# Attention scores of a hybrid encoder block: the queries' high by the keys' low parts over 64 rows of TensorE, two blocks of queries in two halves of its rows

## The chip, the cores and the metric

The kernel runs on one core of a Trainium2 chip. The metric is the device time of one execution in microseconds. A core has five engines that work side by side and wait for one another by semaphores: TensorE (PE in the profile; its weight loads are listed apart, as PEld), VectorE (DVE), ScalarE (ACT), GpSimd (POOL) and SyncE (SP), which issues most DMA transfers. A matrix product on TensorE has a stationary operand, loaded first, of up to 128 rows (the dimension summed over) by 128 columns, and a moving operand of the same rows and up to 512 columns, which streams through. Products are written to PSUM, in banks of 512 f32 a partition.

## What is computed

One layer of a streaming encoder on 512 frames of width 1024: attention and a gated recurrence side by side, merged, then a feed-forward part. The change lies in the attention alone: 16 heads of 64, where each frame sees its own chunk of 64 and the eight chunks before it.

```python
def chunked_band_attention(q, k, v, rel_table):
    ...
    scale = 1.0 / math.sqrt(HEAD_DIM)
    s = jnp.einsum('bnqhd,bnkhd->bhnqk', q, kb).astype(jnp.float32) * scale
    s = s + rel_bias_band(rel_table).astype(jnp.float32)[None, :, None, :, :]
    ...
    s = jnp.where(valid[None, None, :, None, :], s, NEG_INF)
    p = jax.nn.softmax(s, axis=-1).astype(v.dtype)
    o = jnp.einsum('bhnqk,bnkhd->bnqhd', p, vb)
    return o.reshape(B, S, D_ATTN)
```

q, k and v are columns of one projection of the normalised input. All is in float32.

## The kernel before

**High and low parts.** Every matrix product is made of products in the type fp32r. Each operand is split into a high part (the value rounded to fp32r) and a low part (what is left), and a product of two values is high by high, plus high by low, plus low by high; in the big projections (`mm3`, L74) these are three instructions on 128 rows.

**The scores use the rows differently.** A head has only 64 dimensions, so 128 rows hold two things. `q_tile` (L817) projects the queries of two heads (a pair `pr`; head 2·pr+e has the index e) and lays out a tile `q` of 128 x 2 x 512: for head e the rows `own` (0 to 63 for e = 0, 64 to 127 for e = 1) hold the high part of the scaled query, the rows `other` hold its low part. `k_tile` (L828) makes two such tiles: `kh` with the keys' high part in both halves of the rows, `kl` with their low part in both. One product of `q` with `kh` over 128 rows therefore gives high by high plus low by high; one of `q` with `kl` gives high by low plus low by low.

**Scores of a head** (`scores`, L862). The 512 queries are four blocks of 128. Block qb sees the first (qb+1)·128 keys, so its products have 128, 256, 384 and 512 columns. `products(qb)` issues two instructions, L878 with `kh` and L879 with `kl`, into the same place in PSUM. Blocks 0 and 1 share one bank (`low`), block 2 has a bank of the pool `mm` (four banks, used by the projections too), block 3 the second bank with the tag `s`. The products run one block ahead of the softmax: VectorE adds the bias and takes the negative maximum (L887), ScalarE takes the exponential with its sum (L888). After all four blocks VectorE inverts the sums (L889) and GpSimd scales the four blocks (L891).

**Order of the work.** `scores(h + 1)` stands between the transposes of head h's probabilities (`transposed`, L894; ten of 128x128 at L902) and some projections of later heads or gates (`laid`, L934), then the weighting of the values (`weigh`, L911; eight products at L922). So head h+1's softmax runs beside these projections, and TensorE needs the result when it comes to the next transposes. Within this loop TensorE's order is the order of the program (`manual_schedule`); the order on the other engines is made by a planner from its own estimates of durations. Scores of head 0 are issued earlier, while the recurrent branch's output is projected (L950).

**Room.** Tiles of the attention lie in the pools `aw` (values, biases, queries and keys of odd pairs; opened at L846, closed at L978) and `aw2` (probabilities; closed at L965). After that the pool `wo` for part of the output projection's weights is opened (L966). A tile that lies where an older one lay waits until the older one has been read. `halves(e)` (L807) gives the slices `own` and `other`.

Of the kernel before, what the change touches and what calls it, by code (L numbers as in the profile page):

```python
# [9 lines left out]
F32R = mybir.dt.float32r  # L10
# [4 lines left out]
P = 128  # L15
D = 1024
S = 512
KT = D // P
NT = S // P
# [19 lines left out]
def block_kernel(ctx: ExitStack, tc: tile.TileContext, x, norm_mix_g, w_in, b_merge, rel_table,  # L39
# [3 lines left out]
    pe, dve, act, pool, sp = nc.tensor, nc.vector, nc.scalar, nc.gpsimd, nc.sync  # L43

    def pool_of(name, bufs=1, side="left"):
        return tc.tile_pool(name=name, bufs=bufs, side=side, reuse_waits="tile")

    def opened(name, bufs=1, side="left"):
        st = ExitStack()
        return st, st.enter_context(pool_of(name, bufs, side))  # L50
# [17 lines left out]
    def f(ap):  # L68
        return ap.bitcast(F32)

    def mm_tile(name, tag="mm"):
        return ps.tile([P, S], F32, tag=tag, bufs=4 if tag == "mm" else 2, name=name)
# [12 lines left out]
    def split_pair(o, src):  # L85
        split(o[:, 0], o[:, 1], src)
# [249 lines left out]
    def weights(name, ahead=1):  # L336
        prefetch(index[name] + 1 + ahead)
        if index[name] + 1 == len(made):
            low_parts()
        return made[index[name]]  # L340

    def project(o, whl, c, xs, lo=0, hi=S):

        n = len(xs)
        for k in range(n):
            at = slice(c * P, (c + 1) * P)
            mm3(o[:, lo:hi], whl(0, k, at), whl(1, k, at),
                xs[k][:, 0, lo:hi], xs[k][:, 1, lo:hi], k == 0, k == n - 1)
# [165 lines left out]
    low, high = slice(0, S), slice(S, D)  # L514
# [135 lines left out]
    def bias_tile(h):  # L650
        b = aw.tile([P, S], F32, tag="bias", bufs=2, name=f"bias{h}")
        src = ext_d[h:h + 1, 0:S]
        band = bass.AP(tensor=src.tensor, offset=src.offset, ap=[[1, P], [1, S]])
        sp.dma_start(out=b[:], in_=band)
        pool.memset(b[64:128, 448:512], NEG)
        return b
# [144 lines left out]
    def blocks(ap):  # L801
        return ap.rearrange("p (b i) -> p b i", i=P)

    def backwards(ap):
        return blocks(ap)[:, :, ::-1]

    def halves(e):  # L807
        own, other = slice(e * HD, e * HD + HD), slice(HD - e * HD, 2 * HD - e * HD)
        return own, other


    qk = {}

    def qk_pool(pr):
        return aw if pr % 2 else qkp

    def q_tile(pr):  # L817
        po = mm_tile(f"po_q{pr}")
        project(po, weights(f"qk{pr}"), 0, xnT)
        q = qk_pool(pr).tile([P, 2, S], F32R, tag="qk", bufs=3, name=f"q{pr}")  # L820
        for e in range(2):
            own, other = halves(e)
            src = backwards(po[own, :])
            act.activation(blocks(q[own, e]), src, AF.Copy, scale=0.125)
            dve.scalar_tensor_tensor(blocks(q[other, e]), src, 0.125, blocks(f(q[own, e])), ALU.mult, ALU.subtract)
        qk[pr] = [q]

    def k_tile(pr):  # L828
        po = mm_tile(f"po_k{pr}")
        project(po, weights(f"qk{pr}"), 1, xnT)  # L830
        kh = qk_pool(pr).tile([P, 2, S], F32R, tag="qk", bufs=3, name=f"kh{pr}")
        kl = qk_pool(pr).tile([P, 2, S], F32R, tag="qk", bufs=3, name=f"kl{pr}")
        for e in range(2):
            own, other = halves(e)
            act.activation(kh[own, e], po[own, :], AF.Copy)
            dve.tensor_sub(kl[own, e], po[own, :], f(kh[own, e]))
            act.activation(kh[other, e], po[own, :], AF.Copy)
            pool.tensor_copy(kl[other, e], kl[own, e])
        qk[pr] += [kh, kl]

    q_tile(0)
    k_tile(0)
    rw2_stack.close()
    rw_stack.close()
    aw2_stack, aw2 = opened("aw2", 2)
    aw_stack, aw = opened("aw", 2, "right")  # L846


    vs = {}
# [11 lines left out]

    def scores(h):  # L862
        pr, e = divmod(h, 2)
        q, kh, kl = qk[pr]
        bias = bias_tile(h)
        lsum = cp.tile([P, NT], F32, tag="lsum", bufs=2, name=f"l{h}")
        nmax = cp.tile([P, NT], F32, tag="nmax", bufs=2, name=f"m{h}")
        rl = cp.tile([P, NT], F32, tag="rl", bufs=2, name=f"rl{h}")
        prob = [aw2.tile([P, (qb + 1) * P], F32, tag=f"p{qb}", name=f"p{h}_{qb}") for qb in range(NT)]

        low = ps.tile([P, S], F32, tag="s", bufs=2, name=f"s{h}_01")
        scs = [low[:, 0:P], low[:, 256:512], mm_tile(f"s{h}_2"), ps.tile([P, S], F32, tag="s", bufs=2, name=f"s{h}_3")]

        def products(qb):
            w = (qb + 1) * P
            sc = scs[qb][:, 0:w]
            qs = q[:, e, qb * P:(qb + 1) * P]
            pe.matmul(sc, qs, kh[:, e, 0:w], start=True, stop=False, skip_group_check=qb < 2)  # L878
            pe.matmul(sc, qs, kl[:, e, 0:w], start=False, stop=True, skip_group_check=qb < 2)  # L879

        products(0)
        for qb in range(NT):
            w = (qb + 1) * P
            if qb < NT - 1:
                products(qb + 1)

            dve.tensor_tensor_reduce(prob[qb][:], scs[qb][:, 0:w], bias[:, S - w:S], -1.0, 3e38, ALU.add, ALU.min, nmax[:, qb:qb + 1])  # L887
            act.activation(prob[qb][:], prob[qb][:], AF.Exp, bias=nmax[:, qb:qb + 1], scale=-1.0, accum_out=lsum[:, qb:qb + 1])  # L888
        dve.reciprocal(rl[:], lsum[:])  # L889
        for qb in range(NT):  # L890
            pool.tensor_scalar(prob[qb][:], prob[qb][:], rl[:, qb:qb + 1], 1.0, ALU.mult, ALU.mult)  # L891
        return prob
# [41 lines left out]
    def laid(h):  # L934
        m, at = divmod(h, 4)
        qs, ks, va = (lambda pr: lambda: q_tile(pr)), (lambda pr: lambda: k_tile(pr)), (lambda t: lambda: v_tile(m + 1, t))
        if h >= 12:
            return [lambda: gate(0, h - 8)], []
        first_, second = 2 * m + 2, 2 * m + 3
        return {0: (([qs(1), ks(1)] if m == 0 else []) + ([] if m == 0 else [qs(first_)]), [qs(first_)] if m == 0 else []),  # L940
                1: ([ks(first_)], [va(0)]),
                2: ([va(1), va(2)], [va(3)]),
                3: ([qs(second)], [ks(second)])}[at]
# [4 lines left out]
    for j in range(KT):  # L948
        if j == 6:
            prob = scores(0)  # L950
        po = mm_tile(f"po_yb{j}")
        project(po, weights(f"yb{j - j % 2}"), j % 2, rnn)
        dve.scalar_tensor_tensor(zB[j], zB[j], 1.0, po[:], ALU.add, ALU.mult)
    with tc.manual_schedule(engines={mybir.EngineType.PE}):
        for h in range(HEADS):
            pp = transposed(h, prob)
            if h + 1 < HEADS:
                prob = scores(h + 1)
            before, after = laid(h)
            for what in before:  # L960
                what()
            weigh(h, pp)
            for what in after:
                what()
    aw2_stack.close()  # L965
    wo_stack, wop = opened("wo", 4)  # L966
    extra["wo1"] = wop
    barrier[0] = "fg2"
# [3 lines left out]
    for j in range(KT):  # L972
# [2 lines left out]
        dve.scalar_tensor_tensor(ta[j], ta[j], 1.0, py[:], ALU.add, ALU.mult)  # L975
        dve.tensor_add(ta[j], ta[j], zB[j])
        split_pair(mT[j], ta[j])
    aw_stack.close()  # L978
    z_stack.close()
    qk_stack.close()  # L980
    rnn_stack.close()
# [25 lines left out]
    for t in range(NT):  # L1007
# [11 lines left out]
        q = cp.tile([P, 1], F32, tag="ssq", bufs=4, name=f"hsq{t}")  # L1019
# [64 lines left out]
    sc_stack, sc = opened("sc", 2)  # L1084
# [138 lines left out]
    with tc.manual_schedule(engines={mybir.EngineType.PE, mybir.EngineType.DVE}):  # L1223
# [3 lines left out]
        for i in plain:  # L1227
            w = weights(f"fo0_{i}", 3)
# [4 lines left out]
        for n, i in enumerate(paired):  # L1233
            w = weights(f"fo0_{i}", 4)
# [20 lines left out]
        for n, i in enumerate(paired):  # L1255
            w = weights(f"t12_{i}", 4)
# [8 lines left out]
        w = weights(f"fo1_{plain[-3]}", 5)  # L1265
# [75 lines left out]
```

## Time and profile before

| | |
|---|---|
| median of 3 runs | 871.99 us (871.76 to 872.05) |
| profiled execution | 872.03 us |
| its span, first to last instruction | 870.3 us |
| TensorE busy / weight loads busy | 861.0 us / 766.4 us |
| VectorE / ScalarE / GpSimd busy | 599.4 / 488.5 / 100.6 us |
| DMA | 96.39 MB, 111 GB/s in the mean |

Times in the profile are microseconds from the start of the span unless marked ns. A row of the timeline has the start, the duration, the engine, the line of the program, the operation, what is written and read, and the shapes; in brackets stands how long the engine was idle before it, and what ended that. For a product, `128*128 128x512` means 128 rows by 128 columns of weights and a result of 128 partitions by 512. A row of groups gives the count, the busy time, the mean length in ns, then the idle time ahead of the group and who ended it. Products overlap in TensorE's pipeline, so the distance from start to start, and not the length, is what one of them takes of the stream.

### The profile page before, as it was taken

The page shows a single profiled execution, that of the slowest core. Times are in us where ns is not written, and L with a number is a line of the kernel's source. Part 1 is how long each engine was busy: PE and PEld are TensorE (multiplying, and loading weights), DVE is VectorE, ACT ScalarE, POOL GpSimd, SP SyncE. Part 2 cuts the span into 40 slices and gives each one's busy share as a digit, 9 for nine tenths or more (in the row PEclk, how much of TensorE's full clock was granted, in tenths as well). Part 3 has the DMA queues.
Part 4 walks back from the last instruction along what each step waited for, and adds up shares of the span by engine and source line. Part 5 has one row for each costly group of instructions (what it writes and reads, how often), then busy time and mean ns, then how long its engine had stood idle before and what let it go on. Part 6 is the DMA issues. An engine that isn't in the chain of part 4 may idle for free.

```text
span 870.3 us, 13342 instructions
## 1 busy us (share of the span) xinstructions
PE 861.0 (99%) x5130; PEld 766.4 (88%) x5130; DVE 599.4 (69%) x947; ACT 488.5 (56%) x863; POOL 100.6 (12%) x166
## 2 busy tenths in 40 slices
PE   9999999999999999999999999999999999999997
PEld 7988888888889889898888889999999999888885
DVE  5676557563357576775556656988888888698895
ACT  7685546652347576666633366556555556545434
POOL 3602111220012232222200000000000001000000
PEclk9999999999999999999999999999999999999999
DMA  8133223423323232232122802423333332426542
GB/s 285 60 121 97 84 86 97 123 97 96 108 83 89 73 106 89 74 106 76 49 98 101 286 29 72 144 97 122 115 105 97 98 98 76 153 99 233 180 133 96
DMA packets 88735, 96.39 MB, mean 111 GB/s; under 512 B 5744, under 2 KB 74960, under 8 KB 88672
## 3 DMA queue, kind: packets, MB, share of 16 engines
q1 hardware_dynamic: 87072, 92.03, 33.1%
q10 hardware_dynamic: 1232, 2.95, 0.9%
q8 instruction: 40, 0.66, 0.3%
q0 software_dynamic: 368, 0.57, 0.2%
q14 instruction: 23, 0.19, 0.1%
HBM read 93.39 MB, written 2.14 MB: 110 GB/s over the span
## 4 chain that ended last, share of the span: by engine, by line
PE 95%; DVE 2%; DMA 1%; POOL 1%; issue 1%; ACT 0%; SPq 0%; ACTq 0%; DVEq 0%; POOLq 0%
PE po_out L76 2%; PE po_out L77 2%; PE po_out L78 2%; PE p_fu L78 2%; PE p_fg L78 2%; PE p_fg L77 2%; PE p_fg L76 2%; PE p_fu L76 2%; PE p_fu L77 2%; PE pT L902 2%; PE o L922 2%; PE po_v L76 2%; PE po_v L78 2%; PE po_v L77 2%; PE po_xr L77 2%; PE po_gr L78 2%
## 5 line engine op out<-in xcount | busy, mean ns | idle before, releaser
L891 POOL TENSOR_SCALAR p<-p,rl 128x128 f32<-128x128 f32 (+1 forms) x64 | 36.7, 592 | 134.8 <-DVE rl L889 134.5
L888 ACT ACTIVATE p<-p,m 128x128 f32<-128x128 f32 (+1 forms) x64 | 35.7, 560 | 12.1 <-DVE m L887 11.9
L1112 POOL TENSOR_TENSOR act_lo<-act,act_hi 128x1024 fp32r<-128x1024 f32 x1 | 2.4, 2403 | 300.7 <-ACT act_hi L1111 300.7
L76 PE MATMUL po_v<-whl_v,xnT 128*128 128x256 f32 x128 | 36.5, 285 | 0.0
L78 PE MATMUL po_v<-whl_v,xnT 128*128 128x256 f32 x128 | 36.2, 283 | 0.0
L77 PE MATMUL po_v<-whl_v,xnT 128*128 128x256 f32 x128 | 36.2, 283 | 0.0
L76 PE MATMUL po_out<-whl_fo,act_hi 128*128 128x512 f32 (+1 forms) x80 | 30.8, 385 | 0.5 <-ACT c_u L370 0.5
L77 PE MATMUL po_out<-whl_fo,act_hi 128*128 128x512 f32 (+1 forms) x80 | 30.7, 384 | 0.0
L78 PE MATMUL po_out<-whl_fo,act_lo 128*128 128x512 f32 (+1 forms) x80 | 30.7, 384 | 0.0
L83 DVE TENSOR_TENSOR whl_qk<-raw_qk,whl_qk 128x1024 fp32r<-128x1024 f32 x16 | 20.9, 1304 | 13.4 <-ACT whl_qk L82 13.4
L887 DVE CUSTOM_DVE_ANT_0 p<-s,bias 128x128 f32<-128x128 f32 (+1 forms) x64 | 29.1, 484 | 1.0 <-PE s L879 1.0
L83 DVE TENSOR_TENSOR whl_fu_s<-s_fu,whl_fu_s 128x1024 fp32r<-128x1024 f32 x20 | 24.1, 1222 | 6.2 <-ACT whl_fu_s L82 6.2
L83 DVE TENSOR_TENSOR pp<-pT,pp 128x384 fp32r<-128x384 f32 (+1 forms) x48 | 27.6, 597 | 0.5 <-ACT pp L82 0.4
L77 PE MATMUL po_xr<-xnT,whl_xr 128*128 128x512 f32 (+1 forms) x80 | 27.7, 353 | 0.1
L77 PE MATMUL po_gr<-xnT,whl_gr 128*128 128x512 f32 (+1 forms) x80 | 27.5, 347 | 0.0
L78 PE MATMUL po_gr<-xnT,whl_gr 128*128 128x512 f32 (+1 forms) x80 | 27.3, 347 | 0.0
L78 PE MATMUL po_xr<-xnT,whl_xr 128*128 128x512 f32 (+1 forms) x80 | 27.2, 346 | 0.0
L76 PE MATMUL po_gr<-xnT,whl_gr 128*128 128x512 f32 (+1 forms) x80 | 27.2, 347 | 0.0
L83 DVE TENSOR_TENSOR whl_fg_s<-s_fg,whl_fg_s 128x1024 fp32r<-128x1024 f32 x20 | 24.0, 1223 | 4.1 <-ACT whl_fg_s L82 4.0
L82 ACT ACTIVATE whl_qk<-raw_qk 128x1024 fp32r<-128x1024 f32 x16 | 16.9, 1054 | 17.5 <-PE po_yb L78 10.4
L76 PE MATMUL po_xr<-xnT,whl_xr 128*128 128x512 f32 (+1 forms) x80 | 26.3, 351 | 0.3 <-ACT xnT L564 0.2
L76 PE MATMUL po_k<-xnT,whl_qk 128*128 128x512 f32 x64 | 25.2, 393 | 0.0
(498 smaller groups left out, 3258.9 us busy)
## 6 DMA issues: line engine op xcount, KB each, us to landing
raw_fg<-in_w_ffn_in_dram SPq DMA_DIRECT2D x24, 512.0 KB, 4.2
raw_fu<-in_w_ffn_in_dram SPq DMA_DIRECT2D x22, 512.0 KB, 3.6
raw_qk<-in_w_in_dram SPq DMA_DIRECT2D x32, 256.0 KB, 3.2
raw_fo<-in_w_ffn_out_dram SPq DMA_DIRECT2D x16, 512.0 KB, 3.6
raw_xr<-in_w_in_dram SPq DMA_DIRECT2D x8, 512.0 KB, 4.2
raw_gr<-in_w_in_dram SPq DMA_DIRECT2D x8, 512.0 KB, 4.1
raw_ga<-in_w_in_dram SPq DMA_DIRECT2D x8, 512.0 KB, 3.7
raw_gb<-in_w_in_dram SPq DMA_DIRECT2D x8, 512.0 KB, 3.4
```

Source lines behind the costliest of these rows:

```text
L76: pe.matmul(o, sh, mh, start=start, stop=False, skip_group_check=parts)
L77: pe.matmul(o, sh, ml, start=False, stop=False, skip_group_check=parts)
L78: pe.matmul(o, sl, mh, start=False, stop=stop, skip_group_check=parts)
L82: act.activation(hi, src, AF.Copy)
L83: dve.tensor_sub(lo, src, f(hi))
L887: dve.tensor_tensor_reduce(prob[qb][:], scs[qb][:, 0:w], bias[:, S - w:S], -1.0, 3e38, ALU.add, ALU.min, nmax[:, qb:qb + 1])
L888: act.activation(prob[qb][:], prob[qb][:], AF.Exp, bias=nmax[:, qb:qb + 1], scale=-1.0, accum_out=lsum[:, qb:qb + 1])
L891: pool.tensor_scalar(prob[qb][:], prob[qb][:], rl[:, qb:qb + 1], 1.0, ALU.mult, ALU.mult)
L902: pe.transpose(pt[:, at * P:(at + 1) * P], prob[qb][:, kb * P:(kb + 1) * P], ident[:])
L922: pe.matmul(po[:, S - n:S], st, pp[i][:, part, lo:lo + n], start=kb == 0 and part == 0, stop=kb == NT - 1 and part == 1)
L1112: (dve if i else pool).tensor_sub(lo[:], o[:], f(hi[:]))
```

## The change

Queries' high parts are multiplied by keys' low parts over the 64 rows that hold them, instead of all 128, so the product of the two low parts is no longer computed. For block 3 a copy of the queries' high parts, `qh`, is made in the other half of the rows by GpSimd (two copies of 64x128 a pair of heads), and its product uses the other half of TensorE's rows; the low keys are in both halves already. The four high products of a head now come first, then the low ones in the order of blocks 0, 1, 3, 2, and the softmax of the four blocks after all eight. As blocks 0 and 1 share a bank, the high product of block 1 no longer carries the start mark. The pool `aw` is closed before `wo` is opened.

```diff
+        if pr:
+            q_other(pr)
+
+    def q_other(pr):
+
+        q = qk[pr][0]
+        qh = aw.tile([P, P], F32R, tag="qh", bufs=2, name=f"qh{pr}")
+        for e in range(2):
+            own, other = halves(e)
+            pool.tensor_copy(qh[other, :], q[own, e, S - P:S])
+        qhs[pr] = qh
...
     aw_stack, aw = opened("aw", 2, "right")
+    q_other(0)
...
-        q, kh, kl = qk[pr]
+        (q, kh, kl), qh = qk[pr], qhs[pr]
+        own, other = halves(e)
...
-        def products(qb):
-            w = (qb + 1) * P
-            sc = scs[qb][:, 0:w]
-            qs = q[:, e, qb * P:(qb + 1) * P]
-            pe.matmul(sc, qs, kh[:, e, 0:w], start=True, stop=False, skip_group_check=qb < 2)
-            pe.matmul(sc, qs, kl[:, e, 0:w], start=False, stop=True, skip_group_check=qb < 2)
-
-        products(0)
+        def cols_of(qb):
+            return slice(qb * P, (qb + 1) * P)
+
+        def high(qb):
+
+            w = (qb + 1) * P
+            pe.matmul(scs[qb][:, 0:w], q[:, e, cols_of(qb)], kh[:, e, 0:w], start=qb != 1, stop=False, skip_group_check=True)
+
+        def low_(qb, rows, qs):
+
+            w = (qb + 1) * P
+            pe.matmul(scs[qb][:, 0:w], qs, kl[rows, e, 0:w], start=False, stop=True, skip_group_check=True)
+
+        for qb in range(NT):
+            high(qb)
+
+        low_(0, own, q[own, e, cols_of(0)])
+        low_(1, own, q[own, e, cols_of(1)])
+        low_(3, other, qh[other, :])
+        low_(2, own, q[own, e, cols_of(2)])
         for qb in range(NT):
             w = (qb + 1) * P
-            if qb < NT - 1:
-                products(qb + 1)
...
     aw2_stack.close()
+    aw_stack.close()
     wo_stack, wop = opened("wo", 4)
...
-    aw_stack.close()
     z_stack.close()
```

More of the change, by code (lines that the diff above doesn't have):

```diff
@@ L809, in halves @@
         return own, other
-    qk = {}
+    qk, qhs = {}, {}
     def qk_pool(pr):
```

## The prediction, made before the changed kernel ran

> **What bounds the kernel now.** I read the page first: its spans and busy times, then the chain of waits. One execution was profiled: 870.3 us of span, 872.03 us as timed, so 1.7 us lie around the span. That execution stands 0.04 us above the median of the runs (871.99), so a sum made on it holds for the median as it is.
>
> ```profile
> span 870.3 us, 13342 instructions
> PE 861.0 (99%) x5130; PEld 766.4 (88%) x5130; DVE 599.4 (69%) x947; ACT 488.5 (56%) x863; POOL 100.6 (12%) x166
> PE 95%; DVE 2%; DMA 1%; POOL 1%; issue 1%; ACT 0%; SPq 0%; ACTq 0%; DVEq 0%; POOLq 0%
> ```
>
> PE (TensorE) is 95% of the chain that ended last. So a microsecond taken from its stream is a microsecond of the kernel, unless PE then waits for somebody. The windows view over heads 1 to 15 of the attention, and the list of what PE waited for, say how near such waits are:
>
> ```profile
> 244.80:432.00 187.20, 186.31 (x1110) 165.94 (x1108) 122.86 (x269) 123.70 (x270) 44.98 (x87) 1.00 0.29 86
> PE pT L902 <- POOL p L891: 0.9, 3, 0.3
> ```
>
> The columns of the first row are length, then PE, PEld, DVE, ACT, POOL. In 187.20 us PE is idle for 0.89, and that is three waits of at most 0.3 us of the transposes (L902) for POOL's scaled probabilities (L891).
>
> The timeline of PE and of its weight loads (PEld) over one head's scores shows what is to be changed. Columns: start, duration, engine and line.
>
> ```profile
> 304.64 0.19 PEld L878 LDWEIGHTS s<-kh,q 128*128 128x128 f32 x1
> 304.67 0.30 PE L878 MATMUL s<-kh,q 128*128 128x128 f32 x1
> 304.81 0.28 PE L879 MATMUL s<-kl,q 128*128 128x128 f32 x1
> 304.86 0.19 PEld L878 LDWEIGHTS s<-kh,q 128*128 128x128 f32 x1
> 304.93 0.33 PE L878 MATMUL s<-kh,q 128*128 128x256 f32 x1
> 304.98 0.19 PEld L879 LDWEIGHTS s<-kl,q 128*128 128x128 f32 x1
> 305.09 0.28 PE L879 MATMUL s<-kl,q 128*128 128x256 f32 x1
> 305.21 0.34 PE L878 MATMUL s<-kh,q 128*128 128x384 f32 x1
> 305.38 0.33 PE L879 MATMUL s<-kl,q 128*128 128x384 f32 x1
> 305.56 0.39 PE L878 MATMUL s<-kh,q 128*128 128x512 f32 x1
> 305.79 0.40 PE L879 MATMUL s<-kl,q 128*128 128x512 f32 x1
> 305.79 0.19 PEld L76 LDWEIGHTS po_q<-xnT,whl_qk 128*128 128x128 f32 x1
> 306.02 0.40 PE L76 MATMUL po_q<-xnT,whl_qk 128*128 128x512 f32 x1
> ```
>
> Three things are to be seen. From start to start the eight take 0.14, 0.12, 0.16, 0.12, 0.17, 0.18, 0.23 and 0.23 us: 1.35 us a head. A product of 512 columns holds the stream 0.23 us, one of 384 takes 0.17 to 0.18, but one of 128 takes no less than one of 256: 0.12 us, the spacing of the loads (304.86, 304.98), is a floor for each product. And a product is 0.39 us long though its follower starts after 0.23: 0.16 us of it is a tail that the next one covers.
>
> **The change part by part.** *Columns.* The products by the keys' high parts stay at 128 rows, the low ones go to 64; all eight remain, each with its load. The four high ones in a row: 0.14 + 0.12 + 0.17 + 0.23 = 0.66 us. The low ones: 0.12 (block 0), 0.12 (block 1), then block 3 on the other half of the rows and block 2 on its own half. One after the other these two take 0.23 + 0.18 = 0.41. Side by side, with the second begun one load spacing after the first, they take 0.12 + 0.18 = 0.30 (block 3 is through after 0.23). So a head takes 1.20 us where they run together, a gain of 0.15; 1.31 where they don't, a gain of 0.04. Over 16 heads that is -2.4 or -0.6 us. No row shows two products in two halves, so these are the ends that I have for it; I take -2.4, because the only thing that both would need, a load 0.12 after the other, is what the rows show for every pair. If the load for the free half could also be drawn ahead, blocks 1 and 3 would start together: 0.12 + 0.12 + 0.18 = 0.42 instead of 0.54, and -4.3 us.
>
> *The change of rows.* Each head now goes from 128 rows to 64 and back. The trace has one product with few rows, at the start, in the timeline of PE:
>
> ```profile
> 7.57 0.22 PE L464 MATMUL gm_p<-ident,gm_r 8*128 8x8 f32 x1
> 7.72 0.33 PE L562 MATMUL pt_mix_0t<-ident,xs_mix 128*128 128x128 f32 x1
> 7.88 0.27 PE L562 MATMUL pt_mix_0s<-ident,xs_mix 128*128 128x128 f32 x1
> 7.99 0.27 PE L562 MATMUL pt_mix_2t<-ident,xs_mix 128*128 128x128 f32 x1
> ```
>
> The 8-row product ends at 7.79, the 128-row one behind it at 8.05: 0.26 us from end to end. The next two ends, 8.15 and 8.26, are 0.10 and 0.11 apart. So 0.15 us more at the change, which is nearly the tail of 0.16; part of it may be a wait for the data of the second, so this is no proof. Bounds: 0 a change, if the tail is covered as now; 0.16, if the array runs empty first; and if the next weights are not drawn ahead either, another 0.12 to 0.19 (a load's spacing, a load's length). I take 0.15, the row that it is nearest to: 2 x 16 x 0.15 = +4.8 us (0 to 11).
>
> On this the Trainium skill (TensorEngine Tiling, Key Properties) says that a change of tiling mode, unlike a change of tile, drains TensorE. By that alone the term would be the full tail, 2 x 16 x 0.16 = 5.1 us, against 4.8 by the row. The skill (TensorE: Matmul & The Clock Gate, Part 3) also says that a weight load overlaps a running product only where their rows differ; in this trace it does so with the same 128 rows (the load at 304.98 lies inside the product of 304.93), so the measurement decides and the loads of blocks 0, 1 and 2 keep their 0.12.
>
> *The softmax behind it.* The low products used to come right after the high ones; now four high ones go first. VectorE's reduction of block 0 waits for PE:
>
> ```profile
> 305.51 0.29 DVE L887 CUSTOM_DVE_ANT_0 p<-s,bias 128x128 f32<-128x128 f32 x1 [0.34 <-PE s L879]
> 306.07 1.22 DVE L83 TENSOR_TENSOR whl_v<-raw_v,whl_v 128x1024 fp32r<-128x1024 f32 x1
> 310.66 0.18 DVE L889 RECIPROCAL rl<-l 128x4 f32<-128x4 f32 x1
> 311.40 2.05 POOL L891 TENSOR_SCALAR p<-p,rl 128x128 f32<-128x128 f32 x4
> 313.51 0.98 PE L902 MATMUL pT<-ident,p 128*128 128x128 f32 x7 [0.29 <-POOL p L891]
> ```
>
> It began 0.14 us after the end of the second low product (305.09 + 0.28). That one now starts at 304.67 + 0.66 + 0.12, with one row change 0.15 later, and ends at 305.88; the reduction begins at 306.02, 0.51 us late (0.36 without the row change). In this head, and in the two others that wait, VectorE is occupied from there to the reciprocal, POOL follows, and PE stands 0.29 us for the last block. If VectorE keeps its order, the chain moves by 0.51, and PE itself comes 0.15 later (+0.30 for two changes, -0.15 for the overlap): +0.36 a wait. If the planner puts the weight split of 306.07 first, whose cover is 1.22 us, the lateness is gone: -0.15. For three heads -0.45 to +1.1; I take +0.4. No other head's transposes wait (the row of waits counts three).
>
> *POOL, memory, and what costs nothing.*
>
> ```profile
> L838 POOL CAST kl<-kl 64x512 fp32r<-64x512 f32 x16 | 9.8, 610 | 57.9 <-DVE kl L836 57.8
> L655 POOL MEMSET bias<- 64x64 f32 x16 | 2.3, 147 | 9.9 <-DMA bias<-ext_d 9.1
> L82 ACT ACTIVATE whl_wo<-raw_wo x8: 1061/1062/1066, 466.2 to 490.5; 128x1024 fp32r<-128x1024 f32 x8
> L922 PE MATMUL o<-pp,v x128: 220/309/398, 258.1 to 435.8; 128*128 128x512 f32 x32, 128*128 128x384 f32 x32, 128*128 128x256 f32 x32, 128*128 128x128 f32 x32
> ```
>
> The copies of block 3's queries are 16 of 64x128; between a memset of 64x64 (0.147) and a cast of 64x512 (0.610) that is 2.4 to 9.8 us of POOL. They lie in its idle time (45 of 187 us are busy) and are read by the scores two or more steps later, so 0. Without that cover, a copy ahead of a scaled block in one of the two waiting heads that also make queries costs up to 0.61 each, 1.2 us in all. Behind a copy that waits for ACT stand the casts and scalings of POOL, with the same bound. Closing the attention's pool before the output weights' pool is opened lets the latter lie on tiles of the former; the first split of these weights is at 466.2, 30 us after the last product that reads the attention's values (435.8), so 0; without that cover it would cost PE what is missing of it. No transfer is added or moved past another in a queue.
>
> **Sum:** -2.4 + 4.8 + 0.4 = +2.8 us on 872.03: **874.8 us**.
>
> **The rivals.** *No cost at a change of rows* (faster or equal). Its place is the two ends of the 64-row stretch, and it decides below 0.07 us a change. For it: the load of 7.72's product and the product itself start before the modelled end at 7.79. Then PE has -2.4, and -4.3 with the loads drawn ahead. In the three waiting heads the gain is lost and the wait grows by up to 0.36: 0.15 to 0.51 each, 0.5 to 1.5 in all. That gives 870.1 to 871.1, or with loads ahead about 868.7; I put it at 870.2.
>
> *A change also loses the load drawn ahead* (slower). Each of 32 changes then costs 0.12 to 0.19 more, 3.8 to 6.1 us: 878.6 to 880.9. For it: PE draws the next load as the running product starts, and a load that has to fill rows still in use in another form may have to stand back. Against it: the load at 7.72 was not that late.
>
> *The two halves don't run together.* Then the change doesn't do what it says: -0.6 in place of -2.4, so 876.6 with the row changes, 871.4 to 872.5 without them. Against it: nothing in the rows; the two write to different PSUM banks and read different rows.
>
> **How the numbers follow.** About 0.2% (1.7 us) is what a measurement of this kernel can tell from no change, so faster is below 870.3 and slower above 873.7. Forecast (row changes empty the array, halves together or not) 0.36, all slower but 0.01; its own range is 873.0 (0.12 a change, the waits shrinking by 0.45) to 876.9. Loads lost too 0.21, all slower. No cost of row changes 0.34: 0.22 faster (most of it the loads ahead), 0.12 same. Halves apart and changes free 0.09: same. That is faster 0.22, same 0.22, slower 0.56. The range reaches from 869.0, which holds most of the second case but leaves its low end, to 880.0, which leaves the upper part of the third.
>
> **What would show it.** In the changed profile the spacing from the last high to the first low product (now 0.23 at 512 columns) tells a row change: 0.23 is free, 0.38 is the drain, over 0.45 a lost load; so does the start of the product behind the scores. Blocks 3 and 2 starting 0.12 apart, with the next product 0.18 after, would be the overlap; 0.23 apart denies it. The wait of the transposes for POOL (0.9 us, three times) tells the softmax term: about 1.3 if I'm right. I am wrong if a head's eight products take less than 1.30 us up to the next line's start, or more than 1.7.

## The result, and the profile after

The changed kernel takes 874.54 us (median of 8 runs, 874.43 to 874.71) against 871.89 (8 runs, 871.76 to 872.08). The ratio is 1.003, 95% interval 1.0021 to 1.0039: slower by 2.65 us, where 2.8 were forecast. The page of the changed kernel, as before: span, busy times, engines in the chain that ended last.

```profile
span 872.7 us, 13324 instructions
PE 863.2 (99%) x5130; PEld 762.3 (87%) x5130; DVE 600.0 (69%) x947; ACT 489.3 (56%) x863; POOL 104.8 (12%) x182
PE 95%; DVE 2%; ACT 1%; issue 1%; POOL 1%; ACTq 0%; POOLq 0%
```

The span is 2.4 us longer, and PE's busy time 2.2. So TensorE hardly waits longer for others; its own stream has grown. The windows view of the same work as before (the fifteen heads, from 0.04 us ahead of the first transposes) and the list of PE's waits agree: 189.61 us against 187.20, and 0.99 of them idle against 0.89.

```profile
244.76:434.37 189.61, 188.62 (x1109) 162.27 (x1108) 123.73 (x269) 124.38 (x270) 48.92 (x101) 1.00 0.29 85
PE pT L925 <- POOL p L914: 1.0, 3, 0.3
```

The timeline around the scores of the same head as before (5), PE and PEld. Here L893 are the high products and L898 the low ones; `x4` and `x2` stand for merged rows, which reach from the first start to the last end.

```profile
305.00 0.49 PE L925 MATMUL pT<-ident,p 128*128 128x128 f32 x3
305.25 0.89 PE L893 MATMUL s<-kh,q 128*128 128x128 f32 x4
306.06 0.18 PEld L898 LDWEIGHTS s<-kl,q 64*128 64x128 f32 x1 [0.31 <-issue]
306.06 0.32 PE L898 MATMUL s<-kl,q 64*128 64x128 f32 x1
306.07 0.18 PEld L898 LDWEIGHTS s<-kl,qh 64*128 64x128 f32 x1
306.07 0.49 PE L898 MATMUL s<-kl,qh 64*128 64x512 f32 x1
306.23 0.51 PE L898 MATMUL s<-kl,q 64*128 64x256 f32 x2
306.66 0.19 PEld L76 LDWEIGHTS po_q<-xnT,whl_qk 128*128 128x128 f32 x1 [0.19 <-issue]
306.66 0.50 PE L76 MATMUL po_q<-xnT,whl_qk 128*128 128x512 f32 x1
307.00 0.39 PE L77 MATMUL po_q<-xnT,whl_qk 128*128 128x512 f32 x1
```

The start of a product behind a change of rows is noted here when its load begins, so the ends are the better marks, though the profile models them. From the end of the last transpose (305.49) to the end of the first projection product (307.16) there are 1.67 us; before it was 1.51 (from 304.91, the end of the row below, to 306.42).

```profile
304.64 0.27 PE L902 MATMUL pT<-ident,p 128*128 128x128 f32 x1
```

That is 0.16 a head, 2.6 us over 16 heads: nearly the whole loss. Four pieces make it up. What each would be without row changes and overlap is read from the order-only kernel below, which issues the same eight products in the same order on 128 rows:

- The way in. The last high product ends at 306.14, the first low one at 306.38: 0.24 to 0.25, where the order-only kernel has 0.06 (305.40 to 305.46 there). So the way in costs 0.19. The load does not start with the product ahead of it, as the load of the first projection product did before (305.79, with the product of 305.79), but 0.07 us before that one's end. PEld stands idle for 0.31 us without waiting for anybody.
- The overlap. Block 3's load begins 0.01 us after block 0's, and its 512 columns are through at 306.56, before the low products of the other half end at 306.74. It costs the stream nothing.
- The rest of the low products: 306.38 to 306.74, 0.36. The order-only kernel, where block 3 stands in the stream, has 0.58 (305.46 to 306.04), so the overlap is worth 0.22.
- The way out. The last low product ends at 306.74, the first projection product at 307.16: 0.42 to 0.43, where the next one needs 0.23 (307.39). So the way out costs 0.19 to 0.20. Again the load begins 0.07 us before the end of what runs.

Together 0.38 for the pair of row changes, less 0.22 for the overlap: the 0.16 of a head.

### The profile page after: what moved, and what is told of

Read it like the earlier page. It is cut to its first block, busy times and chain, and to the rows that moved or that the text cites. A ratio compares the mean times of both kernels' runs of the same rounds, so it can differ in the third digit from the quotient of the medians.

```text
span 872.7 us, 13324 instructions
## 1 busy us (share of the span) xinstructions
PE 863.2 (99%) x5130; PEld 762.3 (87%) x5130; DVE 600.0 (69%) x947; ACT 489.3 (56%) x863; POOL 104.8 (12%) x182
## 4 chain that ended last, share of the span: by engine, by line
PE 95%; DVE 2%; ACT 1%; issue 1%; POOL 1%; ACTq 0%; POOLq 0%
PE po_out L76 2%; PE po_out L78 2%; PE po_out L77 2%; PE p_fu L78 2%; PE p_fg L78 2%; PE p_fg L77 2%; PE p_fg L76 2%; PE p_fu L76 2%; PE p_fu L77 2%; PE po_v L76 2%; PE o L945 2%; PE po_v L78 2%; PE po_k L76 2%; PE po_v L77 2%; PE po_xr L77 2%; PE po_xr L76 2%
## 5 line engine op out<-in xcount | busy, mean ns | idle before, releaser
L76 PE MATMUL po_q<-xnT,whl_qk 128*128 128x512 f32 x64 | 25.6, 400 | 0.0
```

The source lines that it names most:

```text
L76: pe.matmul(o, sh, mh, start=start, stop=False, skip_group_check=parts)
```

## The experiments

All runs of one group shared a chip and runs of the kernel before, whose median was 871.8 to 871.9 us in each group.

**Block 3 in the same half.** This takes the overlap away and leaves the row changes.

```diff
-        low_(3, other, qh[other, :])
+        low_(3, own, q[own, e, cols_of(3)])
```

> Block 3's low product runs on the own rows too, so nothing runs in the other half; everything else as in the changed kernel. Theory (the two halves run together, and what makes the kernel slower is the price of the two row changes, some 0.34 us a head): block 3's 512 columns now stand in the stream with 0.23 us a head, 16 x 0.23 = 3.7 us, so 878.2 us (877.5 to 879). Rival (the halves never ran together): 874.5 us as the changed kernel.

Measured: 877.61 us, 3.07 over the changed kernel; ratio to the kernel before 1.0065 (1.0052 to 1.0077). The timeline of the same head, four low products on one half:

```profile
306.36 0.89 PE L893 MATMUL s<-kh,q 128*128 128x128 f32 x4
307.18 0.52 PEld L898 LDWEIGHTS s<-kl,q 64*128 64x128 f32 x4 [0.31 <-issue]
307.18 0.90 PE L898 MATMUL s<-kl,q 64*128 64x128 f32 x4
308.01 0.50 PE L76 MATMUL po_q<-xnT,whl_qk 128*128 128x512 f32 x1
```

The low products now reach from 307.18 to 308.08, 0.90 us; in the changed kernel they reached from 306.06 to 306.74, 0.68. So running together is worth 0.22 a head, 3.5 us in all. The total shows 0.4 less. The three waits of the transposes (1.0 us) are gone, probably because a longer stream gives GpSimd the time; the two figures do not add up to the last few tenths. The rival that the halves never ran together falls.

**The order alone.** High products first, low ones after, softmax after all eight, but on 128 rows (`every_row`). The product of the two low parts is computed again.

```diff
+        every_row = slice(0, P)
...
-        low_(0, own, q[own, e, cols_of(0)])
...
+        low_(0, every_row, q[:, e, cols_of(0)])
...
-        low_(3, other, qh[other, :])
+        low_(3, every_row, q[:, e, cols_of(3)])
```

> The changed kernel's order, four high products and then four low ones, but all on 128 rows with both parts of the queries; copies and closing as in the changed kernel. Theory (row changes cost the time): without them and without the overlap a head takes 1.35 to 1.41 us of TensorE, so 871.9 to 873.0 us. Rival (the order, through the later softmax, costs the time): 874 to 875 us, with longer waits of the transposes for POOL.

Measured: 872.57 us, 1.0008 (0.9999 to 1.0017), no difference that is sure. The PE rows of the same head, the last high product and the first low one shown by themselves as well:

```profile
304.17 0.60 PE L926 MATMUL pT<-ident,p 128*128 128x128 f32 x4
304.52 0.88 PE L893 MATMUL s<-kh,q 128*128 128x128 f32 x4
305.01 0.39 PE L893 MATMUL s<-kh,q 128*128 128x512 f32 x1
305.24 0.22 PE L898 MATMUL s<-kl,q 128*128 128x128 f32 x1
305.24 0.80 PE L898 MATMUL s<-kl,q 128*128 128x128 f32 x4
305.88 0.40 PE L76 MATMUL po_q<-xnT,whl_qk 128*128 128x512 f32 x1
```

From 304.77 to 306.28 it is 1.51 us, as before the change. The later start of the softmax is not what costs the 2.65 us. The kernel with block 3 in the same half differs from this one only in the rows of the low products, so the two give the price of the changes: from the end of the last high product to the end of the first projection product this one takes 0.88 us (305.40 to 306.28), that one 1.26 (307.25 to 308.51). That is 0.38 for a pair of changes, as the pieces above gave.

**Row changes without anything side by side.** The kernel before, with each block's low product on the 64 rows, high and low in turn: four ways in and four out per head.

```diff
...
-            pe.matmul(sc, qs, kl[:, e, 0:w], start=False, stop=True, skip_group_check=qb < 2)
+            own, other = halves(e)
+            pe.matmul(sc, q[own, e, qb * P:(qb + 1) * P], kl[own, e, 0:w], start=False, stop=True, skip_group_check=True)
```

> The kernel before, with the low product of each block on the 64 rows of the queries' high part, high and low in turn: eight row changes a head instead of two, nothing side by side. Theory (0.14 us at the way in, 0.20 at the way out): 4 x 0.34 = 1.36 us a head more than before, 16 x 1.36 = 21.8, so 893 us (887 to 897). Rival (fewer rows cost nothing, the order does): 872 us.

Measured: 893.91 us, 1.0252 (1.0238 to 1.0266). That is 22.0 us for 64 pairs of changes, 0.34 a pair, with the columns and the number of products unchanged. The three waits of the transposes (0.9 us) are gone here too, so the changes themselves took about 22.9 us, 0.36 a pair. The first loads of one head show it, no longer 0.12 but 0.26 to 0.31 apart. The last three rows show products of 512 columns, the second at a way in and the third at the way out behind it:

```profile
311.71 0.19 PEld L878 LDWEIGHTS s<-kh,q 128*128 128x128 f32 x1
311.97 0.18 PEld L880 LDWEIGHTS s<-kl,q 64*128 64x128 f32 x1
312.23 0.19 PEld L878 LDWEIGHTS s<-kh,q 128*128 128x128 f32 x1
312.54 0.18 PEld L880 LDWEIGHTS s<-kl,q 64*128 64x128 f32 x1
313.60 0.50 PE L878 MATMUL s<-kh,q 128*128 128x512 f32 x1
314.03 0.49 PE L880 MATMUL s<-kl,q 64*128 64x512 f32 x1
314.45 0.50 PE L76 MATMUL po_q<-xnT,whl_qk 128*128 128x512 f32 x1
```

Their ends, 314.10, 314.52 and 314.95, are 0.42 and 0.43 apart where such a product takes 0.23 without a change. So the way in and the way out cost the same, 0.19 to 0.20.

**Copies and closing alone.** The kernel before with `q_other` and the earlier closing of `aw`; nobody reads the copies.

```diff
+        if pr:
+            q_other(pr)
...
     aw2_stack.close()
+    aw_stack.close()
```

> The kernel before, plus GpSimd's copies of block 3's queries (nobody reads them) and the earlier closing of the attention's pool. Theory (both are hidden): 871.9 us, within 0.4. Rival (GpSimd's queue or the pool's room costs the time): 873 us or more.

Measured: 871.94 us, 1.0001 (0.9992 to 1.001). Both are hidden. In the changed kernel the sixteen copies take 5.7 us of GpSimd, 0.29 in the median, and one of them 1.37.

**Does block 3's early start need its place?**

```diff
         low_(1, own, q[own, e, cols_of(1)])
-        low_(3, other, qh[other, :])
         low_(2, own, q[own, e, cols_of(2)])
+        low_(3, other, qh[other, :])
```

> The changed kernel with the low products in the order of blocks 0, 1, 2, 3. In the changed kernel's trace the load and the product of block 3 begin 7 ns after those of block 0, ahead of block 1, which stands before them in the program. Theory (TensorE draws a product ahead when its half of the rows is free): the same time, 874.5 us (874.2 to 875.0). Rival (the products begin in the order of the program, and block 3's early start needs its place): block 3 begins after block 2, its 512 columns outlast block 2's 384 by 0.06 us and more, so 875.5 to 876.5 us.

Measured: 874.47 us, the same as the changed kernel (874.54). TensorE draws the load and product of the free half ahead of two that stand before it in the program, as the trace of this kernel shows:

```profile
306.09 0.32 PE L898 MATMUL s<-kl,q 64*128 64x128 f32 x1
306.10 0.49 PE L898 MATMUL s<-kl,qh 64*128 64x512 f32 x1
306.26 0.51 PE L898 MATMUL s<-kl,q 64*128 64x256 f32 x2
```

Block 3 (with `qh`) is the last of the four in the program, begins second, and ends at 306.59, before blocks 1 and 2 are through at 306.77.

**Two heads to one stretch.** If a pair of row changes costs 0.34 to 0.38 us and halves run together, a stretch must hold more. With the scores of both heads of a pair in one stretch, the two halves of the rows are filled by two heads, whose queries and keys lie there already.

```diff
+        for qb in range(NT):
+            high(0, qb, qb != 1, False)
+        for qb in range(NT):
+            low_(0, qb, False, True)
+            low_(1, qb, qb != 1, False)
+        for qb in range(NT):
+            high(1, qb, False, True)
...
-            if h + 1 < HEADS:
-                prob = scores(h + 1)
+            if h % 2 and h + 1 < HEADS:
+                probs = scores_of_pair(h // 2 + 1)
```

> The two heads of a pair have their scores in one stretch: four high products of the first, the low ones of both on 64 rows (the first's on rows 0 to 63, the second's on rows 64 to 127, where their high parts lie already, so no copies), then the high ones of the second; scores of a pair at every second head. Theory (a pair of row changes costs 0.34 us, products in two halves run together): 0.72 + 0.14 + 0.64 + 0.20 + 0.64 = 2.34 us a pair against 2.71 before, 8 x 0.37 = 3.0 us less, and the three waits of 0.3 go while one new one of up to 1 us may come at the last pair: 869 us (868 to 870.5). Rival (the later and doubled softmax of the pair decides): 872 us or more, with waits of the transposes.

> As the kernel with two heads at a time, but the low products on all 128 rows with both parts of the queries. Theory: 0.72 + 1.30 + 0.64 = 2.66 us a pair, 0.4 us in all less than before, and the same waits as with 64 rows: 871 to 872 us, 2.5 us over the 64-row version. Rival (taking two heads at a time, by its waits and not by the rows, makes the difference): the same time as the 64-row version.

Measured: 879.88 us (1.0084, 1.007 to 1.0097), and 879.40 with 128 rows (1.0086, 1.0072 to 1.0099). Both miss the expectation by 8 to 11 us. The list of waits of the first, and the timeline of one wait, give the larger part of it; in the 64-row version two stretches of 3.41 us at half the clock add some 3 us, by an estimate from their length (last section):

```profile
PE s L883 <- DVE pp L83: 5.7, 6, 1.3
```

```profile
290.77 0.32 PE L883 MATMUL s<-kl,q 64*128 64x128 f32 x1
292.39 0.96 PE L883 MATMUL s<-kl,q 64*128 64x128 f32 x7 [1.30 <-DVE pp L83]
```

The second head's scores took the two PSUM banks with the tag `t`, which the transposes just before them had filled, and waited until VectorE had split these (7.8 us with 128 rows). It was not the softmax that came late, as the rival had it, but the banks. In the next version the transposes of a pair's second head use one bank of `t` and two of `mm`.

> The kernel with two heads at a time, with the transposes of a pair's second head in one bank of the tag t and two of mm instead of two of t and one of mm, so that the second head's scores find a free bank. In the first version TensorE waited 5.7 us for VectorE's splits of these transposes, and the granted clock fell to a half for 3.4 us twice. Theory (these two took back what the shared row changes gained): without them 879.9 - 5 - 3.4 = 871 to 869 us. Rival (the pair's softmax comes too late wherever the scores lie): 875 us or more, with the wait in the transposes for POOL.

> The same banks with the low products on 128 rows. Theory: 2.5 us over the 64-row version of the same banks (8 pairs of heads, some 0.3 us each), 871.5 to 873 us. Rival (the banks alone matter): as the 64-row version.

Measured: 874.37 us (1.0028, 1.0018 to 1.0039) and 874.40 (1.0029, 1.0017 to 1.004). The banks are better by 5 us and still not free:

```profile
PE s L883 <- DVE pp L83: 2.4, 4, 0.7
```

Neither number came out as expected, and the two versions are equal, although one needs less of TensorE. Its listed waits are longer (2.4 us against 1.8 with 128 rows), which covers only part of the 2.5 us expected between them; the rest is not explained here. The last version puts the pair's scores ahead of those transposes and a projection between, with three buffers for the probabilities instead of two.

```diff
+            if h % 2 and h + 1 < HEADS:
+                probs = scores_of_pair(h // 2 + 1)
+                todo.pop(0)()
             pp = transposed(h, prob)
```

> Two heads at a time on 64 rows as before, but the scores of the next pair stand ahead of the transposes of the pair's second head, with a projection between, so that the transposes' banks are long free; one more buffer for the probabilities; the last four gates are dealt out anew, and the last head's weighting has no cover. Theory: the stream of a pair is 2.40 us (as in the pairs without a wait so far) against 2.71, 8 x 0.31 = 2.5 us less, the three waits of 0.3 go, and about 2 us come at the last head: 870.5 us (869 to 872). Rival (the banks were not what held it, a softmax of two heads always comes late): 874 us or more.

> The same order with the low products on 128 rows: 2.64 us a pair. Theory: 8 x 0.24 = 1.9 us over the 64-row version, 872.4 us (871 to 874). Rival (rows don't matter once two heads share a stretch): as the 64-row version.

Measured: 869.45 us (0.9971, 0.9959 to 0.9982), faster than both kernels, and 871.45 with 128 rows (0.9993, 0.9984 to 1.0002). The 64-row version's wait list has lost the attention's waits but one, of the last head; the timeline of a pair follows, sixteen products:

```profile
PE o L930 <- ACT pp L82: 0.6, 1, 0.6
```

```profile
335.70 0.81 PE L878 MATMUL s<-kh,q 128*128 128x128 f32 x4
336.44 0.91 PE L883 MATMUL s<-kl,q 64*128 64x128 f32 x8
337.28 0.91 PE L878 MATMUL s<-kh,q 128*128 128x128 f32 x4
338.02 0.39 PE L76 MATMUL po_q<-xnT,whl_qk 128*128 128x512 f32 x1
```

The low products of a pair with 128 rows:

```profile
336.91 0.80 PE L878 MATMUL s<-kh,q 128*128 128x128 f32 x4
337.55 1.44 PE L883 MATMUL s<-kl,q 128*128 128x128 f32 x8
```

From the end of the last high product to the end of the last low one, eight low products, 2,560 columns, take 0.84 us in two halves (336.51 to 337.35) against 1.28 on all rows (337.71 to 338.99). The pair takes 2.32 us (335.70 to 338.02), against twice 1.35 before. The 2.0 us between the two versions are what the 64 rows are worth here, 0.25 a pair after the price of two row changes. That agrees with the pieces: one head's four low products, 0.64 us of the order-only kernel's stream, are hidden, and 0.38 goes for the changes.

## Why the prediction was right, step by step

**The sum.** Per head +0.15 of TensorE's stream was forecast (-0.15 and +0.30), +0.16 came, and what was forecast to set the sign did: the row changes cost more than the overlap saves. But both terms were too small, the overlap's -0.15 in place of -0.22 and the changes' +0.30 in place of +0.38. That these misses, a little over 1 us each over 16 heads, cancel is luck.

**The change of rows** was taken at 0.15 from the one product with 8 rows. It measured 0.19 to 0.20 either way, 0.38 a pair; the interleaved kernel gives 0.36. The forecast and its third case were not two cases, as it turned out: the tail is no longer covered, and the next load does wait as well, but it starts 0.07 us before the modelled end of what runs, so both together cost 0.03 to 0.04 more than the tail of 0.16. The same 0.07 stands in the 8-row rows of before: a load at 7.72 with the product ending at 7.79. That load had been read there as a sign that nothing waits; by these runs it was rather a sign that it does. The rule of the Trainium skill (TensorEngine Tiling (Array Packing), Key Properties), that a change of tiling mode drains TensorE, agrees with these runs. By its full tail, 0.16 a change, the prediction had 5.1 us from it; the measured 0.38 a head are 6.1.

**The overlap** was better than the term taken: of the forecast 0.15, 0.11 were the overlap and 0.04 the order, and it saved 0.22. Block 3 started with block 0, not behind block 1; the prediction had kept a start beside block 1 as its lower end (0.42 us for the low products in place of 0.54). What failed is the sentence that a load 0.12 after the other is all that both need: the two halves load side by side (306.06 and 306.07).

**The high products in a row** were put at 0.66, from starts, and all eight in this order at 1.31 without overlap, 0.04 less than before. That gain is not there: the order-only kernel's stretch is 1.51 us, as before the change. Nor is 0.12 us a floor for each product, as the prediction read it: behind 512 columns, the order-only kernel's first low product ends 0.06 after its predecessor. The ends of the high products, which span 0.65 (305.49 to 306.14), can't be held against a sum of starts.

**The softmax** was put at +0.4, between -0.45 and +1.1. The waits rose from 0.9 to 1.0, where the prediction's mark was about 1.3, so this term was 0.3 us too high. The planner did what one bound had supposed: VectorE takes the weight split first.

```profile
306.01 1.49 DVE L83 TENSOR_TENSOR whl_v<-raw_v,whl_v 128x1024 fp32r<-128x1024 f32 x1 [0.26 <-ACT whl_v L82]
307.42 0.28 DVE L910 CUSTOM_DVE_ANT_0 p<-s,bias 128x128 f32<-128x128 f32 x1
311.43 0.18 DVE L912 RECIPROCAL rl<-l 128x4 f32<-128x4 f32 x1
314.30 0.33 PE L925 MATMUL pT<-ident,p 128*128 128x128 f32 x1 [0.33 <-POOL p L914]
```

The wait did not shrink by 0.15, as that bound had it; it went from 0.29 to 0.33. The reciprocal came 0.77 us later than before (310.66), and TensorE, with the loss of the earlier heads, came to this wait 0.75 later (at 313.97, after 313.22).

The order-only kernel, 0.7 us slower than the one before with its interval touching 1, leaves open whether that part is zero.

**The mark given for a row change**, the spacing of starts (0.23, 0.38 or over 0.45), was badly chosen: the starts are 0.33 apart here, as a product is noted from the start of its load. The ends tell it. The other mark, 1.30 to 1.7 us a head, holds: 1.41 from 305.25 to 306.66. Blocks 3 and 2 did not start 0.12 apart, as the mark for the overlap had it; block 3 started with block 0.

**The rivals.** Free row changes are refuted by the interleaved kernel, halves apart by the kernel with block 3 in the same half. What nobody costed is that the same mechanism pays once a stretch serves two heads.

## What to carry to other kernels

Splitting TensorE's rows pays by the stretch, not by the product: here a stretch cost 0.38 us for going in and out, and running one block beside the others gained 0.22, so one head's stretch lost and two heads' stretch won. Before giving a stretch more work, look at which PSUM banks it needs and who has just filled them; a gain of 2.5 us was first buried under waits of 5.7. And read pipelined products by their ends, each against the same product in a kernel that lacks only the change: set against a load's spacing, the way in would have seemed 0.07 cheaper than it is.

## What had not been expected of the hardware

In the first kernel with two heads at a time the granted clock fell to a half for 3.41 us, twice (from 293.52 and from 395.92 us), each time 1.1 to 1.4 us after the end of a wait of 1.3 us inside the 64-row stretch. A third wait of 1.30 us in such a stretch, at 344.23, was not followed by it:

```profile
344.23 0.49 PE L883 MATMUL s<-kl,q 64*128 64x128 f32 x3 [1.30 <-DVE pp L83]
```

The mean granted clock of the five executions was 0.994 in three (879.88 to 880.08 us) and 0.996 in two (878.34 and 878.62 us), so the number of these stretches seems to differ from one execution to the next. The windows view of the first such stretch, with one before and one after (last columns: clock, DMA share, GB/s):

```profile
286.00:290.70 4.70, 4.70 (x41) 4.47 (x39) 2.43 (x4) 3.21 (x5) 0.00 (x0) 1.00 0.02 3
293.60:296.80 3.20, 3.20 (x10) 2.62 (x9) 3.04 (x15) 3.20 (x13) 0.00 (x0) 0.50 0.72 202
297.00:301.00 4.00, 4.00 (x19) 3.31 (x18) 0.18 (x1) 1.00 (x4) 3.85 (x9) 1.00 0.33 86
```

Products of 512 columns came 0.43 us apart in it instead of 0.23. The version with 128 rows waited up to 1.59 us at the same place and kept its clock. Whether the half-filled rows, the wait or both brought it about was not tried.

TensorE also overtakes: with block 3's product last in the program the time was the same, so here a product for a free half of the rows did not wait for those ahead of it in the other half.
